# Starting addresses of a matmul's two SBUF operands, a later take-over of the normed rows, and another spread of the modulation rows, in a four-block transformer kernel on one core

## The chip, the cores and the metric

One NeuronCore of a Trainium2 chip runs the whole program in one launch. The metric is the device time of that launch in microseconds (us); the figure of the kernel before is the median of three executions. One further execution was taken by the hardware profiler, and all rows in this document come from it.

## The reference

All in float32, 256 tokens of width 1024, two blocks of two layers each. The first block's layers run a gated feed-forward, a mixer of four groups, and a second feed-forward, each behind an RMS norm whose scale and shift come from a conditioning vector. The second block puts 16 meta tokens ahead (272 rows) and runs mixer and MLP twice, behind layer norms.

```
cond = silu(c)
mod  = (cond @ ada_w[l] + ada_b[l]).reshape(B, 3, 3, 1, D)      # 9 rows of 1024 a layer: "modulation"
for l in range(2):                                              # first block
    h = rms_norm(x, g[l,0]) * (1 + mod[:,0,1]) + mod[:,0,0]
    a, b = split(h @ ffn1_w13[l]);  x = x + 0.5*mod[:,0,2] * ((silu(a) * b) @ ffn1_w2[l])
    ... mixer (nsa, short conv, gated delta rule, mLSTM) @ w_out[l], gated by mod[:,1,2] ...
    ... second feed-forward, with ffn2_w13, ffn2_w2, mod[:,2,:] ...
for l in range(2):                                              # second block, 272 rows
    h = layernorm(ALPHA*h + mix(h));  h = layernorm(ALPHA*h + square(relu(h @ w1[l])) @ w2[l])
```

## The kernel before

Activations lie transposed: 128 partitions of features by 256 (later 272) columns of tokens. Every large product is split to keep float32 accuracy: the weights arrive by DMA as a raw block of 128x1024 (L140, tiles wraw; the SP queue issues them all in one order, with 4 buffers), ScalarE rounds it to `whi` and VectorE (sometimes GpSimd) forms the rest `wlo` (L153, L154). The activations are split the same way, and each 128x128 step of a product is three matmuls, wh·xh, wh·xl, wl·xh (L170, L171, L172). In such a matmul the weights are the stationary operand (128 columns, loaded while the matmul before runs), and the activations are the moving operand (256 to 274 columns).

Where those operands start is set by the pools that hold them. In the program as built, the stationary block of all but a few of these matmuls starts 64 bytes past a multiple of 256 bytes in its partition, before and after the change. The moving operand starts, past such a multiple: 96 bytes in the first feed-forward; 128 in the other three feed-forwards and in the last MLP; 32 in both mixers; 0 only in the output product of the odd mixer (L2073, tiles yhi and ylo); 0, 64, 128 or 192 by turns in most 272-column products; and some multiple of 8 for the unnormed rows in `vhi`, `vlo`, whose rows are 274 columns long. Counted over the program: 8,384 matmuls of 256 columns start off a multiple of 256 bytes and 472 on one.

At a stage's start the products don't wait for the norm. A feed-forward computes its first `first` feature pairs (m) from the unnormed rows `self.u` in `vhi`/`vlo`, scaled and with two extra columns for the shift (258 columns), and divides afterwards (L386 to L395). Meanwhile `norm` (L346 to L358) makes the normed rows `hhi`/`hlo`: on VectorE one instruction at L353 and one at L356 for each of 8 rows. From m = `first` on products use those rows (256 columns). The MLPs do the same with `AHEAD` blocks (L1723) and `normed_z` (L1671).

Modulation rows: a row of 1024 outputs is 8 raw blocks of 128x1024, each multiplied and summed by one VectorE instruction (L202 or L237). They are streamed beside the weights, in tiles `wada`, through the same SP queue; `ADA_JOBS` says which stage does which rows. In the first feed-forward (`begin` is set) `ada_parts` does this with 3 buffers, and `in_order` holds the DMAs to the order of the code. In that stage the blocks of m = 8 to 21 follow the wide start, one modulation block for each m below 12 and two from 12 on (L456), and two thirds of the `w2` weights have one beside them (L473).

The mixer's generators are interleaved by `weave`, in which each stream has a start and a pace from `PACE`.

Of the kernel before, what the change touches and what calls it, by code (L numbers as in the profile page):

```python
# [17 lines left out]
P = 128  # L18
# [13 lines left out]
SIDE = 9  # L32
W2_CUTS = ((0, 8), (8, 15), (15, 22))

# [46 lines left out]
class Core:  # L81
    def __init__(self, nc, tc, ctx, stream, sizes, cols_ap, cols, rows_ap, rows, ident_ap):
# [8 lines left out]
        self.wp = ctx.enter_context(tc.tile_pool(name="wp", bufs=1))  # L91
        self.pp = ctx.enter_context(tc.tile_pool(name="pp", bufs=1, space=PSUM))
# [12 lines left out]
        self.vhi, self.vlo = (self.keep.tile([P, KD, TN + 2], F32R, name=n) for n in ("vhi", "vlo"))  # L105
# [38 lines left out]
    def h_tiles(self, hp, k, n):  # L144
        return (hp.tile([P, n], F32R, name=f"hhi{k}"), hp.tile([P, n], F32R, name=f"hlo{k}"))
# [29 lines left out]
class Block1(Core):  # L175
# [13 lines left out]
    def ada(self, pool, rows, name="wada", bufs=2, piecewise=False):  # L189
# [4 lines left out]
        for m in range(8):  # L194
            for t, (l, j) in zip(ts, rows):
# [8 lines left out]
                if piecewise or m == 7:  # L204
# [4 lines left out]
                    if kind == 1:  # L209
                        g = self.col(f"g{l}_{s}")  # L210
                        if m == 0 or not piecewise:

                            bg = pool.tile([P, 8], F32, name="bg", bufs=2)
                            nc.vector.scalar_tensor_tensor(bg, self.cols[:, o:o + 8], 1.0, g, op0=ALU.add, op1=ALU.mult)
# [11 lines left out]
    def ada_parts(self, pool, rows, name="wada", bufs=3):  # L226

        nc = self.nc
        for l, j in rows:
# [3 lines left out]
            for m in range(8):  # L233
# [4 lines left out]
                if kind == 1:  # L238
                    g = self.col(f"g{l}_{s}")
                    if m == 0:  # L240

                        bg = pool.tile([P, 8], F32, name="bg", bufs=2)
# [90 lines left out]
    def open1(self, ctx):  # L333

        self.keep1 = ctx.enter_context(self.tc.tile_pool(name="keep1", bufs=1))
        self.work = ctx.enter_context(self.tc.tile_pool(name="work1", bufs=2))
        self.early = [a[:, :, 0:T + 2] for a in (self.vhi, self.vlo)]
# [32 lines left out]
    def ffn(self, l, s, ada1, ada2, begin=None, side=None):  # L370
        nc, tc = self.nc, self.tc
        psum = Banks(self.pp, acc="bbccdd", st="xy", acc2="ddy", late="dd")
        with tc.tile_pool(name=f"fh{l}_{s}", bufs=1) as hp:
# [41 lines left out]
            first = m0 + 4 if begin else 3  # L415
            hs = []

            def place(k):
                if not begin:
                    return self.h_tiles(hp, k, T)  # L420
# [5 lines left out]
            for m in range(m0, FT):  # L426
# [5 lines left out]
                else:  # L432
                    for z in range(2):
                        self.product(ps[z], self.weights(keys(m)[z], z == 1 and m % 2 == 1), x)
                        if begin:
                            next(extra, None)
                if x is self.u:
                    b = hp.tile([P, 2], F32, name="sh", bufs=4)
# [7 lines left out]
                    for _ in range(3 if m >= first - 3 else 0):  # L446
# [5 lines left out]
                if begin:  # L452
# [15 lines left out]
            for m in range(KD):  # L468
# [3 lines left out]
                for k0, k1 in W2_CUTS:  # L472
                    if begin and k0:  # L473
# [45 lines left out]
    def mixer(self, l, ada_jobs=()):  # L519
        nc, tc = self.nc, self.tc  # L520
        psum = Banks(self.pp, pa="b", pc="c", acc="xy", pd="d")
        with tc.tile_pool(name=f"mx{l}", bufs=1) as mx, tc.tile_pool(name=f"mh{l}", bufs=1) as hp:
            self.psum, self.mx, self.l = psum, mx, l
            self.load_rows(mx, f"bsc{l}", f"mng{l}")
# [14 lines left out]
            self.weave([(self.inputs(), 0.0, 1.0), (self.compress(), *PACE["cmp"]), (self.gdn(), *PACE["gdn"]),  # L539
# [1913 lines left out]
```

## Time and profile before

| what | value |
|---|---|
| median of 3 executions | 1978.03 us (1976.43 to 1979.22) |
| the profiled execution, its own time | 1982.88 us |
| its span, first to last instruction | 1981.1 us |
| mean granted TensorE clock | 0.981 |
| stages, us from the span's start | first feed-forward 0 to 254.5 (its weights w2 from 193), mixer to 449.1, feed-forward to 646.6, feed-forward to 835.9, mixer to 1036.1, feed-forward to 1231.4, even mixer to 1353, MLP to 1558.6, odd mixer to 1780, MLP to the end |

The 1.8 us between span and time lie outside the instructions. An engine's busy share says little of what a stage is worth; a busy TensorE is not one at its peak, because a matmul's shown length (0.28 us) covers more than the distance to the next.

### The profile page before, as it was taken

The numbers are of one execution on the slowest core, as the hardware profiler recorded it, in microseconds if no ns is written. First come the engines' busy times: TensorE is split into PE (matmuls) and PEld (weight loads), VectorE is DVE, ScalarE is ACT, GpSimd is POOL, SyncE is SP. The second block draws the span as 40 slices with busy tenths as digits, with TensorE's granted clock in tenths as the row PEclk, the third lists the DMA queues.
The fourth block names the chain that finished last, engine by engine and source line by source line (L and its number), as shares of the span: only waits on it lengthen the run. The fifth ranks groups of instructions, "written<-read, shape, count | busy, mean of one in ns | idle before, by whom it ended". The sixth has DMA issues, their size and how long they took to land.

```text
span 1981.1 us, 39923 instructions
## 1 busy us (share of the span) xinstructions
PE 1899.8 (96%) x16031; PEld 1804.4 (91%) x16031; DVE 1400.4 (71%) x2390; ACT 1005.3 (51%) x1764; POOL 556.9 (28%) x472
## 2 busy tenths in 40 slices
PE   7978999998999999989999999999899999999998
PEld 7878987888999999987898999779899999999998
DVE  7777977568777977977567455779755686578654
ACT  4534474345454544463455444566544465556543
POOL 1242012114531443301124420414431222244402
PEclk9988999999999999999999999999999999999999
DMA  9767955225988798855135766324455544455562
GB/s 356 282 239 272 344 160 188 65 88 171 327 279 255 247 314 284 300 159 182 55 107 182 223 193 195 102 75 161 148 182 171 187 138 157 149 163 171 189 204 96
DMA packets 108808, 384.20 MB, mean 194 GB/s; under 512 B 12076, under 2 KB 14669, under 8 KB 108365
## 3 DMA queue, kind: packets, MB, share of 16 engines
q1 hardware_dynamic: 108620, 381.64, 57.2%
q8 instruction: 126, 2.06, 0.4%
q14 instruction: 62, 0.50, 0.1%
HBM read 379.76 MB, written 1.84 MB: 193 GB/s over the span
## 4 chain that ended last, share of the span: by engine, by line
PE 80%; DVE 10%; DMA 4%; ACT 2%; issue 2%; POOL 1%; SPq 0%; POOLq 0%; DVEq 0%; ACTq 0%
PE acc L170 22%; PE acc L172 21%; PE acc L171 21%; DVE wlo L154 3%; DMA wraw<-in_stream_dram 3%; ACT whi L153 1%; PE b L2049 1%; DVE nt L353 1%; PE pc L961 1%; DMA wada<-in_stream_dram 1%; PE pa L1325 1%; PE acc L770 1%; PE acc L772 1%; PE acc L771 1%; PE pa L1352 1%
## 5 line engine op out<-in xcount | busy, mean ns | idle before, releaser
L153 ACT ACTIVATE whi<-wraw 128x1024 fp32r<-128x1024 f32 (+2 forms) x546 | 563.1, 1037 | 551.1 <-PE acc L171 295.5
L154 DVE TENSOR_TENSOR wlo<-wraw,whi 128x1024 fp32r<-128x1024 f32 (+1 forms) x489 | 624.7, 1284 | 299.4 <-ACT whi L153 292.4
L170 PE MATMUL acc<-hhi,whi 128*128 128x256 f32 (+1 forms) x1824 | 516.6, 288 | 18.5 <-ACT cb L618 5.1
L172 PE MATMUL acc<-hhi,wlo 128*128 128x256 f32 (+1 forms) x1824 | 515.3, 285 | 4.3 <-DVE wlo L154 4.3
L171 PE MATMUL acc<-hlo,whi 128*128 128x256 f32 (+1 forms) x1824 | 516.7, 285 | 1.2 <-POOL hlo L154 1.0
L170 PEld LDWEIGHTS acc<-hhi,whi 128*128 128x128 f32 x1824 | 342.8, 190 | 28.2 <-ACT whi L153 6.4
L172 PEld LDWEIGHTS acc<-hhi,wlo 128*128 128x128 f32 x1824 | 345.2, 190 | 7.4 <-DVE wlo L154 6.5
L171 PEld LDWEIGHTS acc<-hlo,whi 128*128 128x128 f32 x1824 | 346.6, 190 | 5.4 <-POOL hlo L154 2.1
L170 PE MATMUL acc<-g,whi 128*128 128x256 f32 x864 | 246.1, 285 | 16.9 <-ACT whi L153 16.9
L172 PE MATMUL acc<-g,wlo 128*128 128x256 f32 x864 | 245.0, 284 | 1.2 <-DVE wlo L154 1.2
L171 PE MATMUL acc<-g,whi 128*128 128x256 f32 x864 | 245.3, 284 | 0.0
L170 PE MATMUL acc<-vhi,whi 128*128 128x258 f32 (+3 forms) x768 | 220.9, 294 | 11.5 <-ACT whi L153 10.2
L154 POOL TENSOR_TENSOR wlo<-wraw,whi 128x1024 fp32r<-128x1024 f32 x57 | 150.9, 2648 | 263.4 <-ACT whi L153 257.6
L171 PE MATMUL acc<-vlo,whi 128*128 128x258 f32 (+3 forms) x768 | 220.8, 291 | 0.0
L172 PE MATMUL acc<-vhi,wlo 128*128 128x258 f32 (+3 forms) x768 | 216.4, 291 | 3.9 <-DVE wlo L154 3.9
L170 PEld LDWEIGHTS acc<-g,whi 128*128 128x128 f32 x864 | 166.6, 193 | 18.3 <-ACT whi L153 18.3
L172 PEld LDWEIGHTS acc<-g,wlo 128*128 128x128 f32 x864 | 165.8, 192 | 1.9 <-DVE wlo L154 1.9
L171 PEld LDWEIGHTS acc<-g,whi 128*128 128x128 f32 x864 | 166.6, 193 | 0.0
L170 PEld LDWEIGHTS acc<-vhi,whi 128*128 128x128 f32 x768 | 146.8, 193 | 15.6 <-ACT whi L153 10.2
L172 PEld LDWEIGHTS acc<-vhi,wlo 128*128 128x128 f32 x768 | 145.5, 193 | 8.0 <-DVE wlo L154 4.3
L154 POOL TENSOR_TENSOR g<-sb,g 128x256 fp32r<-128x256 f32 x88 | 115.0, 1310 | 126.4 <-ACT g L153 126.2
L171 PEld LDWEIGHTS acc<-vlo,whi 128*128 128x128 f32 x768 | 148.4, 194 | 2.0 <-issue 1.4
(635 smaller groups left out, 3541.7 us busy)
## 6 DMA issues: line engine op xcount, KB each, us to landing
wraw<-in_stream_dram SPq DMA_DIRECT2D x494, 512.0 KB, 4.2
wada<-in_stream_dram SPq DMA_DIRECT2D x136, 512.0 KB, 5.0
wraw<-in_stream_dram SPq DMA_DIRECT2D x64, 448.0 KB, 4.6
g<-in_stream_dram SPq DMA_DIRECT2D x16, 512.0 KB, 8.3
wraw<-in_stream_dram SPq DMA_DIRECT2D x8, 384.0 KB, 3.1
cst<-in_cst_dram SPq DMA_DIRECT2D x1, 1104.0 KB
z<-in_z_dram SPq DMA_DIRECT2D x8, 136.0 KB, 7.2
rows<-in_rows_dram SPq DMA_DIRECT2D x2, 532.0 KB
```

Source lines behind the costliest of these rows:

```text
L153: self.nc.scalar.activation(hi, src, AF.Copy)
L154: (self.nc.gpsimd if pool else self.nc.vector).tensor_tensor(lo, src, hi.bitcast(F32), op=ALU.subtract)
L170: nc.tensor.matmul(ps, wh[:, kw], xh, start=start, stop=False)
L171: nc.tensor.matmul(ps, wh[:, kw], xl, start=False, stop=False)
L172: nc.tensor.matmul(ps, wl[:, kw], xh, start=False, stop=stop)
L353: nc.vector.scalar_tensor_tensor(t, self.x[k], A[:, k:k + 1], self.rstd, op0=ALU.mult, op1=ALU.mult)
L770: nc.tensor.matmul(ps[t], hh[:, tk], wh[:, kw], start=k == 0, stop=False)
L771: nc.tensor.matmul(ps[t], hh[:, tk], wl[:, kw], start=False, stop=False)
L772: nc.tensor.matmul(ps[t], hl[:, tk], wh[:, kw], start=False, stop=k == KD - 1)
L961: nc.tensor.matmul(ps[s, hh], M[s, t, hh], c["eye"][s] if v == 1 else de[t][s, 0, hh], start=True, stop=True)
L1325: nc.tensor.matmul(ps[:, 0:n], qn[z, hh // 2, t * P:(t + 1) * P], keys[b, hh % 2][:, 0:n], start=True, stop=True)
L1352: nc.tensor.matmul(ps[:, hh], PT[hh][:, kb], v[:, kb, b], start=kb == 0, stop=kb == t)
```

## The change

Six edits, all in the same kernel.

1. Addresses: every pool that holds split operands gets a pad in front, tiles are made a multiple of 64 columns wide (`wide`), and small tiles are widened, so that the pairs made by the new `pair` start at multiples of 256 bytes. To make room, a scratch area of the DMA descriptors shrinks from 16,384 to 2,048 bytes a partition. In the program as built 8,064 matmuls of 256 columns then start on a multiple, as do all of 272 and 274 columns and all but 144 of 258; the 576 that remain (432 of 256 columns, 144 of 258) start 64 bytes past one: the queries and gates of the odd mixer, which skip the 16 meta tokens.
2. `first` goes from 3 to 5 in the three later feed-forwards, with two norm rows for each m in place of three; `AHEAD` goes from 11 to 14.
3. The normed rows' split in the MLPs moves from GpSimd to VectorE, and begins one block later.
4. In the first feed-forward modulation blocks have 5 buffers in place of 3, one for each m until 16 and two after (one between the two weights of an m), and 12 in place of 16 beside w2.
5. Row (0,7) moves from there into the first mixer; in the other feed-forwards the modulation blocks begin at m = 5.
6. The first mixer gets its own table of starts and paces.

```diff
+PADS = {"keep": 64, "wp": 64, "work1": 128, "work2": 64, "mx": 224}
+SCRATCH = 2048
+def wide(n):
+    return -(-n // 64) * 64
+def pad(pool, n):
+    pool.tile([P, n // 4], F32, name="pad")
...
-        self.vhi, self.vlo = (self.keep.tile([P, KD, TN + 2], F32R, name=n) for n in ("vhi", "vlo"))
+        pad(self.keep, PADS["keep"])
+        self.vhi, self.vlo = (self.keep.tile([P, KD, wide(TN + 2)], F32R, name=n) for n in ("vhi", "vlo"))
...
-    def h_tiles(self, hp, k, n):
-        return (hp.tile([P, n], F32R, name=f"hhi{k}"), hp.tile([P, n], F32R, name=f"hlo{k}"))
+    def pair(self, pool, name, k, n):
+        return [pool.tile([P, wide(n)], F32R, name=f"{name}{a}{k}")[:, 0:n] for a in ("hi", "lo")]
...
-    def ada_parts(self, pool, rows, name="wada", bufs=3):
+    def ada_parts(self, pool, rows, name="wada", bufs=5):
...
-            first = m0 + 4 if begin else 3
+            first = m0 + 4 if begin else 5
...
                         if begin:
                             next(extra, None)
+                            if z == 0 and m >= m0 + 8:
+                                next(steps)
...
-                    for _ in range(3 if m >= first - 3 else 0):
+                    for _ in range(3 if begin and m > m0 else 2 if not begin else 0):
                         next(normed, None)
...
-                    for _ in range(1 if m < first else 2):
-                        next(steps)
-                else:
-                    a = 8 * len(ada1)
-                    for _ in range((m + 1 - m0) * a // (FT - m0) - (m - m0) * a // (FT - m0)):
+                    next(steps)
+                elif m >= first:
+                    a, n = 8 * len(ada1), FT - first
+                    for _ in range((m + 1 - first) * a // n - (m - first) * a // n):
                         next(steps)
...
-                    if begin and k0:
+                    if begin and (k0 == 8 or k0 and m % 2):
                         next(steps, None)
...
-AHEAD = 11
+AHEAD = 14
...
-            if hp:
-                h = self.h_tiles(hp, k, z.shape[1])
-                self.split(z, *h, pool)
-                self.h.append(h)
+            h = self.pair(hp, "h", k, z.shape[1])
+            self.split(z, *h)
+            self.h.append(h)
...
-                    steps = self.normed_z(gp, True)
+                    steps = self.normed_z(gp)
...
-                if m > 1:
+                if m > 2:
                     next(steps, None)
...
-ADA = (0, 8, 8, 8, 11, 12, 15, 17, 17, 18, 18)
-ADA_JOBS = [[(0, 4), (0, 2), (0, 3), (0, 5), (0, 6), (0, 7)]] + [ROWS[a:b] for a, b in zip(ADA[1:], ADA[2:])]
+ADA = (0, 7, 7, 8, 11, 12, 15, 17, 17, 18, 18)
+ADA_JOBS = [[(0, 4), (0, 2), (0, 3), (0, 5), (0, 6)]] + [ROWS[a:b] for a, b in zip(ADA[1:], ADA[2:])]
...
-    nc = bacc.Bacc("TRN2", target_bir_lowering=False, num_devices=1)
+    nc = bacc.Bacc("TRN2", target_bir_lowering=False, num_devices=1, dynamic_dma_scratch_size=SCRATCH)
```

On the SP queue, in the first feed-forward, the loads for m = 12 to 15 stood so before (wraw are weights, two for an m; wada are modulation blocks; bdram and bt belong to the bias tables):

```order
L140 DMA wada<-in_stream_dram 128x1024
L140 DMA wraw<-in_stream_dram 128x1024 x2
L140 DMA wada<-in_stream_dram 128x1024 x2
L140 DMA wraw<-in_stream_dram 128x1024 x2
L508 DMA bdram<-bv 128x1536
L140 DMA wada<-in_stream_dram 128x1024 x2
L140 DMA wraw<-in_stream_dram 128x1024 x2
L510 DMA bt<-bdram 128x4x256
L140 DMA wada<-in_stream_dram 128x1024 x2
```

and now, to m = 16:

```order
L155 DMA wada<-in_stream_dram 128x1024
L155 DMA wraw<-in_stream_dram 128x1024 x2
L155 DMA wada<-in_stream_dram 128x1024
L155 DMA wraw<-in_stream_dram 128x1024 x2
L526 DMA bdram<-bv 128x1536
L155 DMA wada<-in_stream_dram 128x1024
L155 DMA wraw<-in_stream_dram 128x1024 x2
L528 DMA bt<-bdram 128x4x256
L155 DMA wada<-in_stream_dram 128x1024
L155 DMA wraw<-in_stream_dram 128x1024 x2
L155 DMA wada<-in_stream_dram 128x1024
L155 DMA wraw<-in_stream_dram 128x1024
```

Between two pairs of weights there were two modulation blocks and there is one; from m = 16 on single blocks of both kinds take turns.

On VectorE, where the second feed-forward (449.1 us on) makes its normed rows (nt at L353 is the first half of a row, hlo at L356 the second; se, sh and sb belong to the unnormed pairs; wada is a modulation block), this stood before:

```order
L356 SCALAR_TENSOR_TENSOR hlo_5450<-nt,mod_6_2116,hhi_5449 128x256
L202 SCALAR_TENSOR_TENSOR wada,mod_8_5453<-wada,cond 128x1024
L395 SCALAR_TENSOR_TENSOR sb<-se,sh 128x256
L386 TENSOR_TENSOR se<-acc,rstd 128x256
L444 COPY sh<-acc 128x1
L353 SCALAR_TENSOR_TENSOR nt<-z_74,mod_7_2512,rstd 128x256
L154 TENSOR_TENSOR wlo<-wraw,whi 128x1024
L353 SCALAR_TENSOR_TENSOR nt<-z_75,mod_7_2512,rstd 128x256
```

and now, at the same rows of the norm:

```order
L373 SCALAR_TENSOR_TENSOR hlo_5522<-nt,mod_6_2391,hhi_5521 128x256
L403 TENSOR_TENSOR se<-acc,rstd 128x256
L463 COPY sh<-acc 128x1
L370 SCALAR_TENSOR_TENSOR nt<-z_75,mod_7_3562,rstd 128x256
L170 TENSOR_TENSOR wlo<-wraw,whi 128x1024
L370 SCALAR_TENSOR_TENSOR nt<-z_76,mod_7_3562,rstd 128x256
```

The modulation block is gone from among the norm's rows (three stood there up to the last hlo, none does now), and the work on unnormed pairs goes on for two more m. The tiles z are numbered one higher because a pad stands ahead of them: z_74 and z_75 are the same row.

## Rows read from the trace of the kernel before

**Rows 1.** The page's shares by engine and its slices of 49.5 us.
```profile
PE 1899.8 (96%) x16031; PEld 1804.4 (91%) x16031; DVE 1400.4 (71%) x2390; ACT 1005.3 (51%) x1764; POOL 556.9 (28%) x472
...
PEclk9988999999999999999999999999999999999999
DMA  9767955225988798855135766324455544455562
```

**Rows 2.** The page's chain that ended last, by engine.
```profile
PE 80%; DVE 10%; DMA 4%; ACT 2%; issue 2%; POOL 1%; SPq 0%; POOLq 0%; DVEq 0%; ACTq 0%
```

**Rows 3.** Windows: stretch, length, PE busy (matmuls), clock, DMA share, GB/s.
```profile
1764.00:1776.00 12.00, 12.00 (x108) 1.00 0.56 167
...
590.00:644.00 54.00, 54.00 (x461) 1.00 0.81 259
...
1172.00:1230.00 58.00, 58.00 (x494) 1.00 0.62 187
1880.00:1930.00 50.00, 50.00 (x427) 1.00 0.62 205
```

**Rows 4.** Timeline of TensorE: start and length in us, in two of those stretches.
```profile
1770.04 0.28 PE L172 MATMUL acc<-yhi,wlo 128*128 128x256 f32 x1
1770.16 0.28 PE L170 MATMUL acc<-yhi,whi 128*128 128x256 f32 x1
...
620.00 0.28 PE L172 MATMUL acc<-g,wlo 128*128 128x256 f32 x1
620.12 0.28 PE L170 MATMUL acc<-g,whi 128*128 128x256 f32 x1
```

**Rows 5.** Windows as in group 3, of the other kinds of product.
```profile
195.00:253.00 58.00, 58.00 (x499) 1.00 0.89 321
...
1414.00:1460.00 46.00, 46.00 (x372) 1.00 0.56 184
...
1365.00:1390.00 25.00, 25.00 (x197) 1.00 0.51 168
1786.00:1815.00 29.00, 29.00 (x245) 1.00 0.54 187
```

**Rows 6.** Windows with PE, PEld, DVE, ACT, POOL; then as in group 3.
```profile
10.00:51.00 41.00, 40.81 (x322) 38.38 (x324) 35.09 (x51) 18.65 (x29) 5.65 (x6) 1.00 0.91 361
51.00:76.00 25.00, 24.28 (x215) 17.97 (x214) 18.92 (x41) 11.26 (x17) 0.00 (x0) 1.00 0.94 356
...
118.00:193.00 75.00, 56.90 (x390) 54.71 (x389) 51.28 (x82) 27.52 (x40) 24.60 (x15) 0.82 0.73 275
...
254.50:449.10 194.60, 189.61 (x1904) 164.18 (x1903) 134.25 (x330) 97.73 (x220) 28.47 (x42) 0.98 0.41 130
```

**Rows 7.** Waits of the SP queue, 0 to 260 us: total, times, longest.
```profile
SPq L140 <- DVE wada L237: 99.5, 30, 11.2
```

**Rows 8.** Timeline of the SP queue near 126 us.
```profile
125.90 10.23 SPq L140 DMA_DIRECT2D wada<-in_stream_dram  x2
136.22 0.86 SPq L140 DMA_DIRECT2D wraw<-in_stream_dram  x2
```

**Rows 9.** Windows where normed rows take over, columns as in group 6.
```profile
473.50:490.00 16.50, 13.15 (x92) 12.04 (x91) 13.78 (x25) 7.43 (x14) 3.98 (x3) 0.90 0.53 164
...
1392.00:1412.00 20.00, 14.43 (x90) 12.76 (x89) 12.27 (x23) 9.87 (x23) 10.56 (x10) 0.91 0.18 60
...
1816.00:1829.00 13.00, 9.84 (x78) 9.07 (x77) 10.07 (x19) 8.22 (x16) 6.80 (x8) 1.00 0.28 95
...
1060.00:1077.00 17.00, 14.46 (x114) 13.45 (x113) 13.55 (x22) 8.81 (x16) 6.06 (x4) 1.00 0.38 124
```

**Rows 10.** VectorE's groups by line: count, busy us, mean ns.
```profile
L154 DVE TENSOR_TENSOR wlo<-wraw,whi 128x1024 fp32r<-128x1024 f32 x413 | 544.4, 1324 | 270.9 <-ACT whi L153 264.1 <-PE b L2049 4.8 <-PE acc L171 0.6
L202 DVE SCALAR_TENSOR_TENSOR wada<-wada,cond 128x1024 f32<-128x1024 f32 x80 | 106.0, 1328 | 5.7 <-DMA wada<-in_stream_dram 5.7
...
L154 DVE TENSOR_TENSOR hlo<-z,hhi 128x272 fp32r<-128x272 f32 x8 | 4.3, 550 | 3.9 <-ACT hhi L153 3.9
```

More of the change, by code (lines that the diff above doesn't have):

```diff
@@ L336, in open1 @@
         self.work = ctx.enter_context(self.tc.tile_pool(name="work1", bufs=2))
+        pad(self.work, PADS["work1"])
         self.early = [a[:, :, 0:T + 2] for a in (self.vhi, self.vlo)]
@@ L419, in place @@
                 if not begin:
-                    return self.h_tiles(hp, k, T)
+                    return self.pair(hp, "h", k, T)
                 if k % 2 == 0:
@@ L538, in mixer @@
                                                     self.weights(f"wsc_{l}"), self.u, 28)
-            self.weave([(self.inputs(), 0.0, 1.0), (self.compress(), *PACE["cmp"]), (self.gdn(), *PACE["gdn"]),
-                        (self.gates_mlstm(), *PACE["mlstm"]), (self.conv(), *PACE["conv"]),
-                        (self.nsa(), *PACE["nsa"]),
-                        (self.normed(), *PACE["norm"]), (self.modulation(ada_jobs), *PACE["ada"]), (self.outputs(), *PACE["out"])])
+            self.weave([(self.inputs(), 0.0, 1.0), (self.compress(), *PACE[l]["cmp"]), (self.gdn(), *PACE[l]["gdn"]),
+                        (self.gates_mlstm(), *PACE[l]["mlstm"]), (self.conv(), *PACE[l]["conv"]),
+                        (self.nsa(), *PACE[l]["nsa"]),
+                        (self.normed(), *PACE[l]["norm"]), (self.modulation(ada_jobs), *PACE[l]["ada"]), (self.outputs(), *PACE[l]["out"])])
     def weave(self, streams):
@@ L559, in normed @@
     def normed(self):
-        yield from self.norm(self.l, 1, lambda k: self.h_tiles(self.hp, k, T))
+        yield from self.norm(self.l, 1, lambda k: self.pair(self.hp, "h", k, T))
         self.ready.add("h")
@@ L776, in y_tile @@
     def y_tile(self, m):
-        self.y[m] = (self.hp.tile([P, T], F32R, name=f"hhi{m}"), self.hp.tile([P, T], F32R, name=f"hlo{m}"))
+        self.y[m] = self.pair(self.hp, "h", m, T)
         return self.y[m]
@@ L1597, in open2 @@
         self.work = ctx.enter_context(tc.tile_pool(name="work2", bufs=2))
+        pad(self.work, PADS["work2"])
         self.v = [(self.vhi[:, k], self.vlo[:, k]) for k in range(KD)]
@@ L1781, in even @@
                     nc.vector.scalar_tensor_tensor(v[:, j], v[:, j], self.col(g, j), r, op0=ALU.mult, op1=ALU.mult)
-                    hi = ex.tile([P, TN], F32R, name=f"lhi{first + j}")
-                    lo = ex.tile([P, TN], F32R, name=f"llo{first + j}")
+                    hi, lo = self.pair(hp, "l", first + j, TN)
                     self.split(v[:, j], hi, lo)
@@ L1889, in attend @@
                     return
[L1890 to L1891 removed]
+                hi, lo = self.pair(hp, "y", 4 + pair, TN)
                 nc.scalar.activation(hi, po, AF.Copy)
```

31 lines of the change are left out of this document (15 added, 16 removed).

## The prediction

> **What bounds the kernel now.** I read the page first. TensorE is busy 96% of the span, its clock is full but for a few slices [rows 1], and the chain that ended last runs through it for 80% [rows 2]. So a microsecond is won where matmuls follow each other sooner, or where TensorE stands still. The page can't tell the first of these: a matmul's shown length is 0.28 us, and more than two overlap. What counts is the distance from start to start. I take it from windows in which nothing waits, as (length + 0.28) / count. In four windows of 256-column products at full clock [rows 3] it is:
>
> - 1764 to 1776, the odd mixer's output product: 12.28 / 108 = 113.7 ns;
> - 590 to 644, w2 of a feed-forward: 54.28 / 461 = 117.7 ns;
> - 1172 to 1230, the same elsewhere: 58.28 / 494 = 118.0 ns;
> - 1880 to 1930, the last MLP's second product: 50.28 / 427 = 117.7 ns.
>
> The timeline shows it singly: 0.11 to 0.12 us apart in the first, 0.12 in the second [rows 4]. Both use the same lines, the same weight tiles and the same widths. What differs by the program's addresses is the moving operand's start: a multiple of 256 bytes in the first window, 128 past one in the other three. In the first feed-forward it is 96 past, and the distance there is 58.28 / 499 = 116.8 [rows 5]. DMA share doesn't order them: 0.56 goes with 113.7, 0.62 with 117.7 and 118.0, 0.81 with 117.7 [rows 3]. So I read 4.2 ns a matmul as the price of the offset.
>
> [...] And where normed rows take over, four short windows have far fewer matmuls than fit [rows 9].
>
> **Part A, addresses.** Terms are count x difference.
>
> 1. Moving operands that go from 128 to 0: w2 of three feed-forwards 3 x 528, their w13 from m = 5 on 3 x 816, the last MLP 432 + 768; 5,232 in all, x 4.2 ns = 22.0 us.
> 2. First feed-forward: 528 of w2 and 576 of w13, 116.8 to 113.7: 3.4 us. Its wide start (288) I put at nothing: up to 76 us DMA runs at 356 to 361 GB/s with a share of 0.91 to 0.94 [rows 6], so a faster TensorE meets the loads. If that cover is thinner than it looks, 288 x 4.2 gives 1.2 us more.
> 3. Mixers: 1,056 of 256 columns, x 4.2 = 4.4 us. TensorE waits for others there as well, so half: 2.2.
> 4. The widths 258, 272, 274: 4,188 matmuls, now at 119.5, 124.4 and 128.3 ns (29.28 / 245, 46.28 / 372, 25.28 / 197) [rows 5]. No window shows one of them with all starts on multiples. Below: nothing. Above: as much as the 256-column ones, 4.2 ns each, 17.6 us. I take 1.5 ns, nearer the lower end, because a third of the 272-column ones start on a multiple already, and because rows of these widths aren't a whole number of 256 bytes long wherever they start: 6.3 us.
> 5. The odd mixer's 576 queries and gates stay 64 past a multiple: nothing.
>
> A is 22.0 + 3.4 + 2.2 + 6.3 = 33.9 us, between 25 (terms 1 and 2 alone) and 45.
>
> [...]
>
> **Part B, the first feed-forward's loads.** From 118 to 193 stand 8 pairs, m = 14 to 21, 384 of the 390 matmuls there [rows 6]; at 116.8 they need 44.9 us and take 75, so 30 us go to waiting and to the slow clock. What is late is the weights' load, and what delays it is the queue: SP waited 99.5 us in 30 pieces for wada buffers [rows 7], once 10.2 us before the two weights' loads behind it went out [rows 8]. A wada buffer is free when VectorE has used it, that is behind the pair's own output work, which waits for TensorE; with three buffers and two blocks a pair, the circle closes on itself. After: one block a pair until m = 15, two after, five buffers, so a load waits for work at least two pairs back. Next limit: the loads of m = 16 to 21, four of 512 KB a pair, 5.8 us at 361 GB/s against 48 x 113.7 = 5.5 us of TensorE. That is 2.1 us short over six pairs, and four wraw and five wada buffers hold more than that. VectorE's part of such a pair is 1.5 wlo and 2 blocks, 3.5 x 1.33 [rows 10] = 4.7 us and some small ones: close to full. So I don't take all 30 but 23; between 8 (stalls again at m = 16 to 21) and 30.
>
> Row (0,7) moves to the first mixer: 8 x 1.33 = 10.6 us of VectorE, busy there 134 of 194.6 us, with DMA share 0.41 [rows 6]. It lies beside TensorE's 189.6 us. The new paces reorder streams there. I put both at 2 us lost, between 4 won and 8 lost; without that cover it would be the 10.6.
>
> **Part C, the take-over.** Lost now, window less count x distance [rows 9]: 16.5 - 92 x 117.7 ns = 5.7 us; 17.0 - 114 x 118.0 = 3.5; 20.0 - 90 x 124.4 = 8.8; 13.0 - 78 x 117.7 = 3.8. Together 21.8 us. In the feed-forwards the late thing is VectorE: 16 norm instructions stood among three 1.33 us modulation blocks. Those blocks go, two pairs' small work comes, which evens out; but the rows are due 96 matmuls, 11.3 us, later. So I count 8 of 9.2 us won. In the MLPs the due time moves by 72 matmuls, 9.0 us in the first, while VectorE gets three more wlo (4.0 us), the small work of three more blocks, and 8 x 0.55 [rows 10] for the splits: about 11 us. That eats the delay. What remains is that four blocks' products can fill the wait: I take half, 6 of 12.6 us. C is 14 us, between 4 and 22.
>
> **Sum.** 33.9 + 23 - 2 + 14 = 68.9 us. The profiled execution took 1982.9 us (its span and 1.8 us around it, which nothing here changes); less 68.9 that is 1914.0. The median of the three runs is 4.9 us below it, so the forecast for the median is 1978.0 - 68.9 = 1909.
>
> **Rivals.**
>
> - The offset isn't what makes 113.7 (10%). The fast window is one stage, and something else there could be the reason. Against it: the last MLP's second product has the same shape, weights from the same buffers and nearly the same DMA share (0.62 against 0.56), and takes 117.7. A falls out: 1978 - 35 = 1943. [...]
> - The first feed-forward stays late (18%): VectorE, nearly full from m = 16, holds the wada buffers again, B wins 5 in place of 23: 1927. For it: 3.5 x 1.33 us of a 5.5 us pair. Against it: from m = 16 on half of the blocks stand between a pair's two weights, ahead of its output work.
> - Slower (3%): the load of the next weights gets in the way of the moving operand's reading. By the program's addresses the next weights will start 64 bytes past it, modulo 512, in 7,780 of the 256-column matmuls; in the fast window that distance is 320. If 64 is worse, 8,064 matmuls pay. B, C and the mixer give 35 back, so it turns slower from 35 / 8064 = 4.3 ns above today's 117.7, that is over 122.0 ns. At 126 it would be 1978 - 35 + 67 = 2010. No row shows this distance alone; against it speaks only that of the distances shown none takes over 118.0.
> - It doesn't do what it says for 576 matmuls, which is counted above and is worth 2.4 us.
>
> **Numbers.** My forecast has 69%; 1909 is its time. Its parts' bounds give 25 + 8 - 8 + 4 = 29 at worst and 45 + 30 + 4 + 22 = 101 at best; all at one end is unlikely, and taking in the second rival and the edge of the first gives 1884 to 1943. A change of under 0.2% couldn't be told from none here. Faster 0.95, same 0.02, slower 0.03: only the third rival ends above 1978, and several shortfalls together would be needed for no change.
>
> **What would show it.** Distances of 113 to 114 ns in windows of every 256-column w2 and last-MLP product (A right; near 118 wrong); 272-column ones near 123; granted clock above 0.95 from 118 us to the end of w13 in the first feed-forward, and SP's wait for wada under 40 us (B); full counts where normed rows take over in the feed-forwards, and some loss left in the first MLP (C); the first mixer at 190 to 197 us. It would be wrong if the wide start or the streaming stages turn out bound by loads: DMA share near 0.95 with TensorE waiting.

## The result, and the profile after

The changed kernel took 1913.12 us (median of four runs, 1906.31 to 1919.59) against 1978.03: a ratio of 0.967, interval 0.964 to 0.971. In a later set of runs, beside other runs of before, it took 1909.24 us (1906.07 to 1910.70), ratio 0.966, interval 0.964 to 0.967. The forecast was 1909, in a range of 1884 to 1943. The profiled execution is the slowest of the first four (1919.59, a span of 1917.8), so it stands against the 1982.9 of before with 63.3 us won.

The page of the changed kernel: busy time, clock and DMA by slices, and the chain that ended last ([rows 1, 2] before).
```profile
PE 1858.6 (97%) x16031; PEld 1766.7 (92%) x16031; DVE 1417.6 (74%) x2442; ACT 1005.7 (52%) x1764; POOL 552.4 (29%) x456
...
PEclk9999999999999999999999999899999999999999
DMA  9879656326987799754236765234455544454562
...
PE 82%; DVE 11%; DMA 2%; issue 2%; ACT 2%; POOL 1%; POOLq 0%; SPq 0%; DVEq 0%; ACTq 0%
```
The low clock of the first feed-forward is gone from the slices, TensorE's share of the chain went from 80 to 82%. The bound is the same as before.

Where the time went, by stages. A stage runs from its first product to the next stage's first; the numbers are differences of start times in the traces of before, of the changed kernel, and of the changed kernel in the second set (us):

| stage | before | after | after, second set |
|---|---|---|---|
| first feed-forward, from the span's start | 254.5 | 227.2 | 225.2 |
| first mixer | 194.6 | 195.4 | 196.8 |
| second feed-forward | 197.5 | 190.3 | 184.6 |
| third feed-forward | 189.3 | 182.1 | 182.2 |
| second mixer | 200.2 | 196.6 | 193.4 |
| fourth feed-forward | 195.3 | 184.6 | 186.2 |
| even mixer | 121.6 | 120.2 | 114.8 |
| first MLP | 205.6 | 199.3 | 198.9 |
| odd mixer with its output | 221.4 | 221.4 | 221.5 |
| last MLP, to its last product | 189.0 | 188.3 | 188.1 |

Windows of the changed kernel where nothing waits, columns as in [rows 3]: length, PE, PEld, DVE, ACT and POOL busy (counts), clock, DMA share, GB/s. They are w2 of the first, second, third and fourth feed-forward, the odd output, and two of the last MLP's second product; the eighth has 272 columns.
```profile
175.00:225.00 50.00, 50.00 (x443) 50.00 (x443) 43.50 (x65) 25.52 (x36) 8.96 (x8) 1.00 0.81 280
560.00:610.00 50.00, 50.00 (x427) 50.00 (x427) 38.04 (x45) 23.93 (x33) 8.41 (x8) 1.00 0.79 255
740.00:790.00 50.00, 50.00 (x444) 50.00 (x443) 46.05 (x65) 24.64 (x34) 4.50 (x6) 1.00 0.96 343
1120.00:1170.00 50.00, 50.00 (x443) 50.00 (x442) 28.33 (x36) 22.02 (x28) 0.00 (x0) 1.00 0.64 197
1680.00:1692.00 12.00, 12.00 (x108) 12.00 (x108) 9.25 (x15) 6.26 (x11) 5.34 (x6) 1.00 0.29 93
1820.00:1865.00 45.00, 45.00 (x385) 45.00 (x383) 23.68 (x23) 18.10 (x18) 2.94 (x4) 1.00 0.63 201
1873.00:1893.00 20.00, 20.00 (x179) 20.00 (x178) 11.70 (x15) 11.67 (x19) 6.35 (x7) 1.00 0.42 134
1402.00:1442.00 40.00, 40.00 (x326) 40.00 (x326) 20.88 (x20) 16.36 (x20) 4.75 (x5) 1.00 0.60 194
```
By the prediction's formula, (length + 0.28) / count, the steps are 113.5, 117.8, 113.2, 113.5, 113.7, 117.6, 113.3, and 123.6 for the 272 columns. A step is the time from one matmul's start to the next one's, which the prediction calls a distance; from here on a distance is one of bytes. The formula counts whole matmuls, so a window can be off by some 0.2 ns. So not every aligned 256-column product came to 113: the second feed-forward and most of the last MLP stayed at 117.8, with moving operands on multiples of 256 bytes like the others. DMA share doesn't sort them: 113.2 stands beside 0.96 and 117.8 beside 0.79. Inside a stretch the step is one or the other for hundreds of matmuls. The second feed-forward begins at 113 and changes once. The steps from 456.1 us on, in ns, from the trace:
```
113 113 114 112 114 114 113 113 114 115 120 117 118 118 118 117 118 118 (and so on for 1,324 matmuls)
```

The first feed-forward's pairs from m = 14 on, then the take-over of normed rows in the second, third and fourth feed-forward and in the two MLPs, same columns; and SP's wait for wada buffers from 0 to 260 us ([rows 6, 7, 9] before).
```profile
118.00:165.60 47.60, 45.21 (x386) 44.21 (x386) 47.37 (x66) 20.74 (x35) 27.67 (x16) 1.00 0.85 312
...
445.00:470.00 25.00, 25.00 (x213) 25.00 (x212) 24.57 (x36) 14.77 (x25) 12.70 (x8) 1.00 0.62 194
...
628.00:650.00 22.00, 22.00 (x189) 22.00 (x188) 20.40 (x35) 12.97 (x21) 9.75 (x8) 1.00 0.62 189
1010.00:1030.00 20.00, 20.00 (x171) 20.00 (x170) 19.57 (x39) 13.42 (x25) 9.28 (x7) 1.00 0.48 159
1340.00:1365.00 25.00, 21.66 (x167) 20.64 (x166) 21.53 (x39) 17.41 (x35) 11.38 (x9) 1.00 0.41 134
1750.00:1775.00 25.00, 21.94 (x180) 21.17 (x180) 21.72 (x48) 16.43 (x32) 9.71 (x7) 1.00 0.38 127
...
SPq L155 <- DVE wlo L170: 60.7, 34, 5.4
SPq L155 <- DVE wada L253: 21.8, 17, 5.0
```
In the first feed-forward the same work takes 47.6 us in place of 75, at full clock (1.00 in place of 0.82), and SP waits 21.8 us for wada buffers in place of 99.5. Its wait for VectorE's other work, wlo, grew to 60.7 us from 27.0, but the weights come early enough all the same: from 118 to 165.6 us TensorE waited 2.3 us in all, for wlo. In the three feed-forwards TensorE does not stand still at the take-over. In the MLPs it still does: 25.28 - 167 x 123.6 ns = 4.6 us, and 25.28 - 180 x 117.8 ns = 4.1 us. Before, by the same formula, it was 9.1 and 4.1 (the prediction's 8.8 and 3.8 leave out the 0.28).

### The profile page after: what moved, and what is told of

It is laid out like the page before. It is cut to its first block, busy times and chain, and to the rows that moved or that the text cites. A ratio compares the mean times of both kernels' runs of the same rounds, so it can differ in the third digit from the quotient of the medians.

```text
span 1917.8 us, 39932 instructions
## 1 busy us (share of the span) xinstructions
PE 1858.6 (97%) x16031; PEld 1766.7 (92%) x16031; DVE 1417.6 (74%) x2442; ACT 1005.7 (52%) x1764; POOL 552.4 (29%) x456
## 4 chain that ended last, share of the span: by engine, by line
PE 82%; DVE 11%; DMA 2%; issue 2%; ACT 2%; POOL 1%; POOLq 0%; SPq 0%; DVEq 0%; ACTq 0%
PE acc L186 22%; PE acc L188 22%; PE acc L187 22%; DVE wlo L170 3%; DVE wada L253 1%; PE b L2066 1%; DMA wraw<-in_stream_dram 1%; ACT whi L169 1%; DMA wada<-in_stream_dram 1%; PE pa L1344 1%; PE pc L980 1%; PE acc L789 1%; PE acc L790 1%; PE acc L791 1%; PE pc L998 1%
## 5 line engine op out<-in xcount | busy, mean ns | idle before, releaser
L186 PE MATMUL acc<-hhi,whi 128*128 128x256 f32 (+1 forms) x1680 | 475.5, 286 | 9.1 <-ACT cb L637 4.7
L187 PE MATMUL acc<-hlo,whi 128*128 128x256 f32 (+1 forms) x1680 | 474.6, 283 | 3.7 <-DVE hlo L170 3.7
L188 PE MATMUL acc<-hhi,wlo 128*128 128x256 f32 (+1 forms) x1680 | 473.3, 283 | 4.5 <-DVE wlo L170 4.5
L186 PEld LDWEIGHTS acc<-hhi,whi 128*128 128x128 f32 x1680 | 316.1, 189 | 16.8 <-ACT cb L637 5.1
L187 PEld LDWEIGHTS acc<-hlo,whi 128*128 128x128 f32 x1680 | 319.0, 190 | 7.4 <-DVE hlo L170 4.6
L188 PEld LDWEIGHTS acc<-hhi,wlo 128*128 128x128 f32 x1680 | 318.1, 189 | 7.0 <-DVE wlo L170 5.6
L186 PE MATMUL acc<-vhi,whi 128*128 128x258 f32 (+3 forms) x912 | 259.7, 290 | 11.8 <-ACT whi L169 10.5
L187 PE MATMUL acc<-vlo,whi 128*128 128x258 f32 (+3 forms) x912 | 259.3, 288 | 0.0
L188 PE MATMUL acc<-vhi,wlo 128*128 128x258 f32 (+3 forms) x912 | 255.0, 288 | 4.0 <-DVE wlo L170 4.0
L186 PEld LDWEIGHTS acc<-vhi,whi 128*128 128x128 f32 x912 | 173.3, 192 | 15.9 <-ACT whi L169 10.5
L170 POOL TENSOR_TENSOR g<-sb,g 128x256 fp32r<-128x256 f32 x88 | 117.5, 1340 | 103.7 <-ACT g L169 103.7
```

The source lines that it names most:

```text
L170: (self.nc.gpsimd if pool else self.nc.vector).tensor_tensor(lo, src, hi.bitcast(F32), op=ALU.subtract)
L186: nc.tensor.matmul(ps, wh[:, kw], xh, start=start, stop=False)
L187: nc.tensor.matmul(ps, wh[:, kw], xl, start=False, stop=False)
L188: nc.tensor.matmul(ps, wl[:, kw], xh, start=False, stop=stop)
```

## The experiments

After the first trace there were two theories of the 113 ns. Theory 1 is the prediction's: a moving operand that starts on a multiple of 256 bytes can run at 113. Theory 2 adds that two steps are possible there, and that the start of a stretch settles which. The rivals stand in the expectations.

**The addresses alone.** The changed kernel with the old schedule: the hunks on the first feed-forward's loads, the take-over, the paces and the row (0,7) undone.
```diff
-def ada_parts(self, pool, rows, name="wada", bufs=5):
+def ada_parts(self, pool, rows, name="wada", bufs=3):
...
-AHEAD = 14
+AHEAD = 11
...
-ADA = (0, 7, 7, 8, 11, 12, 15, 17, 17, 18, 18)
+ADA = (0, 8, 8, 8, 11, 12, 15, 17, 17, 18, 18)
```


> The changed kernel with the old schedule: addresses as after, everything else (first feed-forward's modulation loads, take-over of normed rows, paces and row (0,7)) as before. Theory 1 (a moving operand that starts on a multiple of 256 bytes can run at 113 ns, one that does not runs at 117.7): stretches of 256-column products at 113 to 114 ns appear in places where before had 117.7, though not in all, since the changed kernel kept 117.8 in its second feed-forward too. By the base times of the changed kernel's stages addresses gave about 25 us there, so 1953 us (1944 to 1960). Rival (the starts do nothing, something else made the fast stretches): 1978 us.

It took 1953.41 us against 1974.57 of before beside it, ratio 0.989 (0.987 to 0.991): 21.2 us. In its windows, w2 of the third feed-forward, m = 14 to 21 of the first, and the first mixer:
```profile
760.00:810.00 50.00, 50.00 (x444) 50.00 (x443) 45.33 (x73) 25.89 (x42) 3.77 (x5) 1.00 0.93 326
...
118.00:191.40 73.40, 55.27 (x384) 53.51 (x385) 48.16 (x77) 26.98 (x39) 24.02 (x15) 0.81 0.72 277
251.30:443.20 191.90, 186.98 (x1903) 161.31 (x1903) 134.03 (x329) 97.19 (x219) 28.48 (x41) 0.99 0.41 131
```
The third feed-forward is at 113.2, but the waiting from 118 us on is as in [rows 6]. The first feed-forward ends at 251.3 in place of 254.5, so addresses gave 3.2 us there; and the first mixer, with the old paces, takes 192.0.

**The moving operands at 128.** Four pads.
```diff
-PADS = {"keep": 64, "wp": 64, "work1": 128, "work2": 64, "mx": 224}
+PADS = {"keep": 192, "wp": 192, "work1": 192, "work2": 128, "mx": 224}
```


> The changed kernel with four pads larger, so that nearly all moving operands start 128 past a multiple of 256 bytes and the weights stay 64 past one; the schedule is the changed one. Theory 1: no stretch of 256-column products under 117 ns, the odd mixer's output product included (113.7 in both kernels until now), and the time is 1913 plus about 27 us = 1940 us (1934 to 1948). Rival (a stretch's distance comes from how it starts, whatever the address): stretches at 113 ns remain and the time stays at 1913 us.

1938.01 us (1935.69 to 1939.31), ratio 0.981 (0.979 to 0.984), 25 to 29 us above the changed kernel's two medians. Windows of w2 of the third feed-forward, and of the first MLP's 272 columns:
```profile
747.00:797.00 50.00, 50.00 (x427) 50.00 (x427) 45.18 (x64) 23.50 (x32) 3.76 (x5) 1.00 0.93 332
...
1420.00:1460.00 40.00, 40.00 (x318) 40.00 (x317) 19.32 (x18) 15.10 (x16) 2.12 (x4) 1.00 0.55 184
```
117.8 ns, in every feed-forward and in the odd output too; 126.7 for the 272 columns. One thing fits theory 1 badly: some hundred matmuls in short stretches behind stops (46 in a row at the last MLP's take-over, from 1786.4 us) ran at 113.3 all the same. So the short step is rare at 128, not impossible.

**The first feed-forward's loads as before.**
```diff
-                            if z == 0 and m >= m0 + 8:
-                                next(steps)
...
-                    next(steps)
+                    for _ in range(1 if m < first else 2):
+                        next(steps)
...
-                    if begin and (k0 == 8 or k0 and m % 2):
+                    if begin and k0:
```
with three wada buffers.

> The changed kernel with the first feed-forward's loads of modulation weights as before: two blocks a pair from m = 12 on, none between a pair's two weights, a block ahead of each later cut of w2, three buffers in place of five. Theory (these loads held up the weights' loads): the stretch from 118 us to w2 loses about 25 us again, SP waits 80 to 100 us for the buffers, 1938 us (1932 to 1944). Rival (aligned starts or the removed row had closed the gap, the buffers matter little): under 10 us lost, below 1923 us.

1940.71 us (1935.04 to 1951.02), 28 to 31 us lost by the medians, where the profiled execution was the slowest and had the second and the fourth feed-forward at 117.8. Its first feed-forward shows the effect by itself; the window is m = 14 to 21 there, the second row SP's wait from 0 to 260 us:
```profile
118.00:191.70 73.70, 57.14 (x384) 55.37 (x385) 47.52 (x78) 27.34 (x40) 24.31 (x15) 0.79 0.74 275
...
SPq L155 <- DVE wada L253: 90.4, 23, 10.6
```
It ends at 251.6 us, against 227.2 and 225.2: the loads are worth 24.4 to 26.4 us at the changed addresses. With the moving operands at 128 and the new loads it ends at 228.9, so the gain does not hang on the addresses.

**The take-over as before.**
```diff
-            first = m0 + 4 if begin else 5
+            first = m0 + 4 if begin else 3
...
-AHEAD = 14
+AHEAD = 11
...
-                steps = self.normed_z(gp)
+                steps = self.normed_z(gp, True)
```
and the modulation blocks from m = 0 on.

> The changed kernel with the take-over of normed rows as before: from m = 3 in the feed-forwards with modulation blocks among the norm's instructions, from m = 11 in the MLPs with POOL doing part of the splits. Theory (TensorE waited for the norm there): the losses at the take-over come back, 13 us in the three feed-forwards and 4 in the first MLP by the two traces, 1930 us (1924 to 1936). Rival (the losses moved for other reasons, the faster matmuls or the paces): within 5 us of 1913.

1924.05 us (1923.28 to 1934.24), 11 to 15 us lost. Its second feed-forward happened to run at 113 throughout, so its stage compares with the second set's: 189.6 against 184.6 us. At its take-over:
```profile
440.00:460.00 20.00, 16.44 (x133) 15.44 (x132) 18.10 (x34) 10.44 (x20) 6.23 (x4) 1.00 0.59 179
```
20.28 - 133 x 118 ns = 4.6 us stood still. The third feed-forward lost 1.4 us, the fourth 3.4 to 5, the first MLP (its first product 106.5 us against 103.7 and 103.3) 3, the last MLP nothing.

**The changed kernel again.** Nothing edited.

> The changed kernel once more, unchanged. In the first execution of it that was profiled, aligned 256-column products ran at 113.3 ns in some stages and at 117.8 in others (all of the second feed-forward from m = 5 on), with the same code and the same kind of addresses. Theory 2 (two distances are possible for aligned operands; what happens where a stretch begins, or a hiccup of some ns in it, settles which, and it then lasts until the next stop): stages can change their distance from one execution to another, which also gives the 13 us between the four times, and a switch inside a stage stands next to a step that is out of line. Rival (the distance belongs to the stage, by its buffers or its queue): the same stages at the same distances, each to 0.3 ns. Time 1906 to 1920 us by both.

1909.24 us. The second feed-forward, in w2, and the even mixer's middle, in this execution and in the first one:
```profile
550.00:600.00 50.00, 50.00 (x444) 50.00 (x443) 40.75 (x61) 25.22 (x41) 4.83 (x5) 1.00 0.84 289
...
1228.40:1238.40 10.00, 10.00 (x65) 7.76 (x66) 7.81 (x30) 6.63 (x18) 2.42 (x3) 1.00 0.17 55
```
```profile
1236.20:1246.20 10.00, 10.00 (x45) 6.94 (x44) 4.49 (x22) 4.30 (x14) 1.51 (x2) 0.63 0.01 2
```
The second feed-forward ran at 113.2 this time, 5.7 us shorter: the step is the execution's, not the stage's. And the even mixer, 5.4 us shorter, kept its full clock, where the first execution had 0.63 in ten microseconds, with 0.50 from 1233.6 to 1243.4 us, and 0.83 and 0.86 in two windows before. Up to then the two executions had done the same: in the last ten microseconds ahead of the first drop (from 1186.2 and 1178.4 us) TensorE was busy 8.62 and 8.54 us with 65 matmuls in each, at a clock of 1.00. Why the clock fell in one of them alone stays open. The second feed-forward and the even mixer make 11 of the 13.6 us between the two spans.

**A stop put in on purpose.**
```diff
+    def again(self, ps):
+        with self.tc.issue_after(self.last(mybir.EngineType.PE)):
+            self.nc.tensor.matmul(ps, self.ones, self.z[0][:, self.z[0].shape[1] - T:], start=True, stop=True)
...
+                if not begin and m == 8: self.again(st())
...
+                if out_ap is not None and m == 19:
+                    self.again(pair([P, n]))
```


> The changed kernel with one more product of ones and a block of z, in 32-bit floats and 256 columns, whose result nobody reads, ahead of m = 8 in the second to fourth feed-forward and ahead of m = 19 in the last MLP's first product; in the first kernel's traces stretches that began behind such a product ran at 113.3 ns seven times in seven. Theory 2: the stretches behind it run at 113.3 ns to the end of w2 in every feed-forward, and in the last MLP to m = 6 of the second product: 1,200 matmuls of the second feed-forward and 800 of the last MLP x 4.5 ns = 9 us won, four products of 0.4 us lost, 1905 us, with less spread between executions (under 6 us). Rival (the distance belongs to the stage): the second feed-forward stays at 117.8 and the time is 1914 or 1915.

1913.48 us (1910.32 to 1917.63): nothing won; the last MLP took 1.6 us less, and the other three stops won nothing. Windows of the second feed-forward's w2 and of the last MLP behind m = 19:
```profile
555.00:605.00 50.00, 50.00 (x427) 50.00 (x427) 37.51 (x52) 24.00 (x34) 5.35 (x6) 1.00 0.80 267
1780.00:1810.00 30.00, 30.00 (x267) 30.00 (x266) 18.14 (x21) 15.72 (x30) 14.89 (x12) 1.00 0.58 194
```
The last MLP went from 117.8 to 113.4 behind the product, as theory 2 had it, but the second feed-forward came to it at 117.8 and left it at 117.8. The first steps behind it, in ns, of the second and of the third feed-forward, whose products are the same:
```
117 119 117 118 118 118 117 118
117 117 123 118 113 114 113 113
```
Both left the stop as they had come to it, the third at 113.4, and so did the fourth; of four stops one changed the step. So a stop can change the step but need not, and nothing found in the program tells which way it goes.

**The weights at 0 and at 128.** Two kernels; the moving operands stay on multiples.
```diff
-PADS = {"keep": 64, "wp": 64, "work1": 128, "work2": 64, "mx": 224}
+PADS = {"keep": 64, "wp": 0, "work1": 160, "work2": 96, "mx": 224}
```
and "wp": 128, "work1": 96, "work2": 32.

> The changed kernel with three pads changed, so that the weights start on a multiple of 256 bytes (64 past one in both kernels until now) and the moving operands stay on multiples. Theory 1 (the moving operand's own start counts): 113.3 ns in as many stretches as before, 1913 us (1904 to 1922). Rival (what counts is the distance between the weights' start and the moving operand's): another distance in all 256-column products, no stretch at 113.3, 1935 us or more.

> The changed kernel with three pads changed, so that the weights start 128 past a multiple of 256 bytes and the moving operands stay on multiples. Theory 1: 113.3 ns in as many stretches as before, 1913 us (1904 to 1922). Rival (the distance between the two starts counts): 128 apart is what neither kernel had; no stretch at 113.3, 1935 us or more.

1955.48 us (1953.78 to 1956.39) and 1948.07 us (1946.33 to 1951.09), 35 to 46 us above the changed kernel. w2 of the third feed-forward, weights at 0 and then at 128:
```profile
752.00:802.00 50.00, 50.00 (x419) 50.00 (x419) 44.70 (x65) 23.31 (x32) 3.76 (x5) 1.00 0.95 328
```
```profile
750.00:800.00 50.00, 50.00 (x423) 50.00 (x422) 45.10 (x64) 23.46 (x32) 3.74 (x5) 1.00 0.94 332
```
120.0 and 118.9, and no long stretch at 113 in any stage. From start to start the means are 120.0 in every stage with the weights at 0, and 118.7 with the weights at 128, where two stretches (150 matmuls of the first feed-forward and 190 of the last MLP) ran at 120.0. Theory 1 fell: the moving operands had kept their starts. What had changed is how far the moving operand starts past the weights, modulo 256 bytes: 192 in the changed kernel (0 less 64), 0 and 128 here. With the weights at 128 the odd mixer's queries and gates (moving at 64 past) came to 192, and their mean step went from 119.7 to 114.9. With the weights at 0 they came to 64, and it went to 117.8. This made theory 3: the distance between the two starts counts.

**Both 128 further.** One pad, in front of weights and moving operands alike.
```diff
-PADS = {"keep": 64, "wp": 64, "work1": 128, "work2": 64, "mx": 224}
+PADS = {"keep": 192, "wp": 64, "work1": 128, "work2": 64, "mx": 224}
```


> The changed kernel with one pad larger by 128 bytes, which moves the weights and the moving operands together: nearly no moving operand starts on a multiple of 256 bytes any more, but the weights stand 64 behind them as in the changed kernel. Theory 3 (formed on the two runs that moved the weights: what counts is the distance from the weights' start to the moving operand's, modulo 256 bytes; 192 allows 113.3 ns, 0, 64 and 128 give 120.0, 117.8 and 118.7): stretches at 113.3 as in the changed kernel and 1911 us (1903 to 1922). Theory 1 (the moving operand's own start on a multiple): 117.7 everywhere, 1938 us or more, as when the moving operands alone stood at 128.

1908.48 us (1905.23 to 1912.30), ratio 0.967 (0.964 to 0.970): as the changed kernel, with the moving operands at 128 and the weights at 192, so almost no moving operand on a multiple of 256. w2 of the fourth feed-forward:
```profile
1115.00:1165.00 50.00, 50.00 (x443) 50.00 (x443) 28.36 (x35) 22.02 (x28) 0.00 (x0) 1.00 0.63 196
```
113.5 ns. Theory 3 holds against theory 1 here too.

**Distances of 160 and 224.** The weights at 96 and at 32, each with a pad of 32 bytes ahead of the work pools to keep the moving operands in place.
```diff
-PADS = {"keep": 64, "wp": 64, "work1": 128, "work2": 64, "mx": 224}
+PADS = {"keep": 64, "wp": 96, "work1": 96, "work2": 32, "mx": 224}
...
+        pad(self.keep1, 32)
```
and "wp": 32, with the rest as it was.

> The changed kernel with the weights at 96 past a multiple of 256 bytes in place of 64, moving operands on multiples: a distance of 160 modulo 256. By theory 3 the distance is what counts, and 160 lies between 128 (118.7 ns, never under 117) and 192 (113.3 or 117.8). If the good distances reach to it, 1911 us or, if the longer step does not occur there, 1905; if not, 118 ns or more everywhere, 1940 to 1950 us. Theory 1 (the moving operand's start alone) has fallen, by it the time would be 1911 us.

> The changed kernel with the weights at 32 past a multiple of 256 bytes in place of 64, moving operands on multiples: a distance of 224 modulo 256. The kernel before had some 500 matmuls at this distance, in its mixers, with 118.3 ns on average and a twentieth of them short. Theory 3, read from these: about 118 ns everywhere, 1935 to 1945 us. If only their broken stretches made them slow, the short step occurs here as at 192: 1905 to 1915 us.

1936.19 us (1931.49 to 1942.79) and 1943.70 us (1943.17 to 1944.55). At 160, w2 of the third and of the fourth feed-forward; then at 224, the third:
```profile
748.00:798.00 50.00, 50.00 (x423) 50.00 (x423) 45.51 (x66) 23.30 (x32) 4.04 (x5) 1.00 0.94 332
1137.00:1187.00 50.00, 50.00 (x428) 50.00 (x427) 27.07 (x33) 21.34 (x26) 0.00 (x0) 1.00 0.62 193
```
```profile
748.00:798.00 50.00, 50.00 (x425) 50.00 (x424) 45.09 (x62) 24.03 (x32) 3.76 (x5) 1.00 0.94 335
```
118.9 and 117.5 at 160 (118.7 and 117.3 from start to start), 118.3 at 224: neither has a stretch at the short step. The good distance doesn't reach to the next 32 bytes on either side.

**The odd mixer at 192, and one stop.** The rows that it reads start 192 bytes into their tiles, and the stop ahead of m = 19 in the last MLP alone.
```diff
-    def pair(self, pool, name, k, n):
+    def pair(self, pool, name, k, n, o=0):
...
-                    steps = self.normed_z(hk)
+                    steps = self.normed_z(hk, 48)
```


> The changed kernel with two additions. (1) The rows that the odd mixer reads start 192 bytes later in their tiles, so that its 432 queries' and gates' products of 256 columns stand at a distance of 192 from the weights (0 in the changed kernel, 119.7 ns), and its 432 keys' and values' products of 272 columns at 128 (192 until now). Theory 3 (the distance modulo 256 counts): 256 columns at 113.3 to 115, which wins 2.2 to 2.7 us; 272 columns 2 to 3 ns longer, by the other kernels' means at 128 and 192, which loses 0.9 to 1.3. (2) One product of ones and z that nobody reads, ahead of m = 19 in the last MLP: where the restart kernel had it, 800 matmuls ran at 113.4 in place of 117.8, 3.6 us, for 0.5 lost. Together 1906 us (1900 to 1912) against 1909 to 1913 of the changed kernel's two sets of runs; only the windows can tell so small a gain from its spread. Rival (the distance has no part in the odd mixer's 119.7): its products stay at 119 to 120 and the time at 1907 to 1911.

1914.26 us (five runs, 1904.35 to 1915.81), ratio 0.968 (0.966 to 0.971): no gain that can be told. In the profiled execution the odd mixer without its output took 0.8 us less than in the second set, its 256-column steps falling to 114.8 on average from 119.7 as theory 3 says. The last MLP ran at 113.4 behind the stop, as this window shows, but it had been there before the stop too (from m = 18 on), and it fell back to 117.8 in the second product's next block, so that the whole stage won 0.3 us:
```profile
1770.00:1800.00 30.00, 30.00 (x267) 30.00 (x267) 17.10 (x22) 16.68 (x31) 13.13 (x12) 1.00 0.57 192
```
So 1.1 us came of the 4 to 5 that the expectation's terms make, and the executions differ by more than either.

## Why the prediction was right, and where it wasn't

**The sum.** 68.9 us were forecast; 64.9 came in the first set, 68.9 in the second. The parts, though, were not what they were taken for. Nor do those below add up to the whole: 21.2, 24 to 26, 13 to 14 and the mixer's 2 to 6 lost make 52 to 59. The 21.2 is a difference of medians; in the traces the kernel with the addresses alone is 29.3 us shorter than before, whose profiled execution lay 4.9 us above its median, and with 29.3 the parts make 60 to 67, against 63.3 and 76.9 between the traces of before and of the changed kernel.

**Part A, 33.9 forecast (25 to 45), 21.2 measured** by the addresses alone (29.3 by the traces). The step that failed is the reading of [rows 3]: "what differs by the program's addresses is the moving operand's start". The weights stood at the same 64 past a multiple in all four windows, so start and distance to the weights could not be told apart there. Five kernels tell them apart: with both moved the 113 stays, with the weights alone moved it goes, at four other positions of them. The edit gave the right distance, since it put the moving operands at 0 while the weights stood at 64. That multiples of 256 bytes were the right place for them is luck: with the weights at 0 as well the kernel takes 1955 us.

The sizes, term by term. (1) 22.0 was forecast for 5,232 matmuls, all short. In the first profile the third and fourth feed-forward were, 2,688 x 4.4 ns = 11.8 us, and about 240 of the last MLP, 1 us; the second feed-forward's 1,344, 5.9 us, came in the second set alone. That the short step is possible and not certain is what the prediction missed. (2) 3.4 forecast, 3.2 measured at the end of the stage. (3) 2.2 forecast for both mixers together; with the old paces the first took 2.6 less and the second 2.7, so this was too small. (4) 6.3 forecast; the 272 columns went from 124.4 [rows 5] to 123.6, the 258 columns from 119.5 to 120.3 in the second set (a window of 15 us with 127 in the last MLP), which cancels most of it; the 274 columns went from 127.9 to 126.6 on average. What holds for 256 columns need not for 258: with the moving operands at 128 these took 118.4 (129 in 15 us). (5) Nothing forecast, nearly right, though these did not stay where they were: before, the queries and gates stood at distances of 0, 64, 128 and 192 by turns, after at 0, and the mean step of the 432 with 256 columns went from 118.3 to 119.7, 0.6 us lost.

**Part B, 23 forecast (8 to 30), 24 to 26 measured**, with the mechanism as written: SP's wait, the clock (1.00, where the trace of before has four stretches of over 6 us at 0.50) and the count show it, and undoing these edits alone brings all three back. VectorE was busy 47.4 of 47.6 us there, so the second rival's ground was real, and yet its cost didn't come: SP's wait for wada stayed at 21.8, and the longer wait for wlo (60.7) held TensorE up little (2.3 us).

**First mixer, 2 us lost forecast (4 won to 8 lost).** 192.0 with the old paces and row (addresses alone), 193.5 to 198.0 in the kernels that have the new ones at the same distance: 2 to 6 lost. No run tells the row from the paces.

**Part C, 14 forecast (4 to 22), 13 to 14 measured.** The feed-forwards gave 10 to 11, not 8 (1.4 of it in the third, which the prediction left out), and the MLPs 3, not 6: the last MLP's wait stayed, 4.1 us before and after. That fits the prediction's reckoning that the longer work ahead eats the later due time; no run parts the two, nor edit 2 from edit 3.

**The rivals.** That the offset doesn't make the 113 is half true: the offset alone doesn't, the distance does. For 256 columns the runs show 113.3 to 120.0 ns, by address alone. The third rival named the right quantity, the weights' start against the moving operand's, and feared the wrong value: weights 64 bytes past the moving operand (the distance of 192 in these runs) is the one of seven distances with long stretches at the short step, and a multiple of 256 more or less changed nothing (320 in the odd output of before, 113.7; 64 in that of the changed kernel, 113.7 too). The cause that it gave, a load in the way of a reading, no run shows. Whether a matmul's own weights count or those loaded for the next one can't be told, since nearly all of them start alike modulo 256.

**Open.** What settles which step a stretch takes was not found. In the last MLP the long step came at m = 18 in five of the six profiled executions with this distance and the new take-over; in the second feed-forward it came and went between executions. A gap of the same kind, with the same products behind it, led to either.

## What to carry to other kernels

When TensorE is the bound, measure the step from start to start in windows without waits, and set it against the byte distance between the start of the moving operand and that of the weights, for each width by itself; some pads of 32 to 128 bytes were worth 21 to 46 us of 1,913 here. In a trace of one layout, look for what else is constant before naming the cause: the start and the distance were one and the same thing until a run moved one of them. And look at two executions before reading a difference of a few microseconds in a stage: 11 us of this kernel come and go with a step and a clock.

## What the runs showed of the hardware

Steps of split 256-column products at full clock, means from start to start in the traces, by the moving operand's start less the weights', modulo 256 bytes:

| distance | step, ns | from |
|---|---|---|
| 0 | 120.0 | weights at 0 |
| 32 | 116.7 | first feed-forward of before |
| 64 | 117.8, rarely 113.3 | before, moving operands at 128 |
| 128 | 118.7, rarely 120.0 | weights at 128 |
| 160 | 117.3 or 118.7, by stretch | weights at 96 |
| 192 | 113.3 or 117.8, by stretch | the changed kernel, both 128 further |
| 224 | 118.3 | weights at 32 |

The odd mixer's queries and gates, which start 64 bytes further than the rest, follow the same table at other places (means of 404 steps in each kernel): 119.7 at 0, 116.9 at 32, 117.8 at 64, 118.6 at 128, 114.9 at 192 and 118.3 at 224.

Not expected was that one distance can have two steps. At 192 either lasted for over a thousand matmuls in the changed kernel's first trace: 1,341 at 113.3 in the third feed-forward, 1,324 at 117.8 in the second. There the change to 117.8 came with no stop, at steps of 115 and 120 ns, and of the four stops put in one changed the step. The kernels at distances with one step nearly everywhere had narrow spreads (1.4 us at 224, 2.6 at 0, 3.6 at 64), and the widest belong to distances with two (11.3 us at 160, 13.3 in the changed kernel's first set). But the addresses alone, at 192, spread over 2.8 us, and before, with one step nearly everywhere, over 10.7 in one set of seven, so the two steps are not all of it.
